# A step of the RWKV-7 recurrence on one core: four state products together, output products and the next first products queued behind them

## The chip, the cores and the metric

The kernel runs on one core of a Trainium2 chip. The metric is the device time of one execution in microseconds (us). Five engines work side by side, each through its own instructions in order, and meet through semaphores: PE (TensorE, matmuls; its weight loads are listed as PEld), DVE (VectorE), ACT (ScalarE), POOL (GpSimd) and SP (SyncE, which issues the transfers). Only PE writes products, into PSUM; DVE and ACT take them from there.

## The reference

Two decoder layers over 1024 tokens of width 1024. Layer 0 mixes time with the RWKV-7 recurrence, 16 heads of 64 by 64 state; layer 1 attends with a forget gate. Each has an MLP of squared ReLU behind it. The recurrence is what the change touches:

```python
def step(S, inp):
    r_t, w_t, k_t, v_t, a_t, b_t = inp
    sa = jnp.einsum('bhvk,bhk->bhv', S, a_t)
    S = S * w_t[:, :, None, :] + sa[..., :, None] * b_t[..., None, :] + v_t[..., :, None] * k_t[..., None, :]
    y = jnp.einsum('bhvk,bhk->bhv', S, r_t)
    return S, y
...
x = x + (1.0 + gt1) * y
h = modulate(rms_norm(x, norm_mlp_g[i]), sh2, sc2)
x = x + (1.0 + gt2) * sq_relu_mlp(h, mlp_up[i], mlp_down[i])
```

## The kernel before, in words

The recurrence is done in chunks of 64 tokens. A unit (`units`) is four heads (two pairs, `q` = 0 and 1; `e` = 0 and 1 are the two heads of a pair) over 256 tokens, so four chunks; there are 16 units, and so 64 steps `c`. What can be had without the state is made ahead by `early` and `late` for the units to come. The rest is serial, and it is `chain`. A step of it has five kinds of product, four small matmuls (64 columns) each, one for each `q` and `e`; letters are used for them from here on:

- **A**: state by the decayed keys, into a tile `pq` (line 888; a helper's line, so rows show it as L875 `pq<-st,ar` or `pq<-sv,ar`). DVE adds `xk` and writes `xs` (line 892).
- **Y**: state by the receptance, into the output bank `py` (line 890; L875 `py<-ar,st`).
- **T**: the solved triangle `tt` by `xs`, into `pq` (line 897; L875 `pq<-xs,tt`). ACT and DVE copy the halves to `uv` (lines 898, 899).
- **B**: the new part of the state, `bkt` by `uv`, into `pq` (line 906). DVE scales it and adds the decayed old state (lines 908 and 910), one instruction for each `q`; POOL makes the decayed copy `sp` for the next step (line 867).
- **O**: the part of the output from within the chunk, `uv` by `sc`, into `py` (line 915).

The trace shows each of these matmuls as two records: x8 in one of its rows are the four matmuls of one kind in a step.

`pq` is one bank with one buffer: each new product into it waits for the reader of the last. In the code of before, the loop over `q` holds two B's and then DVE's update of that `q`, twice over. The steps of the recurrence are short, so other work is put between them: at each `yield` of `chain`, `units` runs a few pieces of the preparation, of the gating of the unit before and of dense work (`beside`: projections, then the MLP of the first 512 tokens). `tc.issue_after` queues these pieces behind the chain's instruction on its engine. The dense work is `mm3` (lines 124, 126, 128): three matmuls of 512 columns for a product, on weights that `load_w` brings and splits in two (lines 115 to 117). A scheduler sets the final order of each engine's instructions from priorities and these edges; the chain has high priority, which lets its ready instructions go first but doesn't hold two of them together.

Of the kernel before, what the change touches and what calls it, by code (L numbers as in the profile page):

```python
# [75 lines left out]
class K:  # L76
# [596 lines left out]
    def phase_wkv(self, es, rest, done):  # L673


        tc, nc, ap = self.tc, self.nc, self.ap
        V, S, G, PE = nc.vector, nc.scalar, nc.gpsimd, nc.tensor
        ident = self.cst("ident")
        H = (slice(0, 64), slice(64, 128))
# [3 lines left out]
        def where(u):  # L683

            j, g, q = u // 8, u % 8 // 2, u % 2
            return j, 2 * g, slice(j * HT + q * 256, j * HT + (q + 1) * 256)
# [5 lines left out]
        def lng(n, shape, bufs=2):  # L692
            return pool["s"].tile(shape, F32, name=n, tag=n, bufs=bufs)
# [4 lines left out]
        def bank(n, bufs=1):  # L698
            return (self.pe if n == "pe" else pool["p"]).tile([128, 512], F32, name=n, tag=n, bufs=bufs)
# [151 lines left out]
        def chain(u, w):  # L851

            j, p, ts = where(u)
            ar, uv, sc, xk, bkt, tt, pc = (w[n] for n in ("ar", "uv", "sc", "xk", "bkt", "tt", "pc"))
            yp = bank("py")
            old = self.sv[:, p:p + 2]
            begin, end = ts.start == 0, ts.stop == T
            of = lambda a: a.rearrange("p (q c) d -> p q c d", q=2)
            pc, xk = pc.rearrange("p (q c) -> p q c", q=2), of(xk)
            us = [of(uv[0:64, :, e]) for e in range(2)]  # L860

            def small(n, bufs=2):
                return lng(n, [128, 2, HD], bufs)

            def scaled(st, c):
                sp = small("sp")
                G.tensor_tensor(out=sp, in0=st, in1=pc[:, :, c:c + 1].broadcast_to([128, 2, HD]), op=ALU.mult)
                return sp

            def state():  # L870
                return bank("pq")[:, 0:128].rearrange("p (q d) -> p q d", q=2)

            def both(ps, lhs, rhs, start, stop):
                for e in range(2):
                    ins = PE.matmul(out=ps[H[e]], lhsT=lhs[H[e]], rhs=rhs[H[e]], start=start, stop=stop)  # L875
                return ins


            st = None if begin else old
            sp = None if begin else scaled(old, 0)  # L880
            for c in range(4):
                first, last = begin and c == 0, end and c == 3
                ys = [yp[:, (q * 4 + c) * HD:(q * 4 + c + 1) * HD] for q in range(2)]
                xs = xk[:, :, c]
                if not first:
                    ps = state()
                    for q in range(2):
                        ins = both(ps[:, q], ar[:, 0, q * 4 + c], st[:, q], True, True)
                    for q in range(2):
                        both(ys[q], st[:, q], ar[:, 1, q * 4 + c], c + q == 0, False)  # L890
                    x = small("xs")
                    ins2 = V.tensor_tensor(out=x, in0=ps, in1=xs, op=ALU.add)
                    xs = x
                    yield ins, ins2
                ps = state()
                for q in range(2):
                    ins = both(ps[:, q], tt[:, q * 4 + c], xs[:, q], True, True)
                S.copy(out=us[0][:, :, c], in_=ps[H[0]])
                yield ins, V.tensor_copy(out=us[1][:, :, c], in_=ps[H[1]])
                ins2 = None  # L900
                if not last:
                    ps = state()
                    st = small("st", 3) if c < 3 else old
                    for q in range(2):
                        for e in range(2):
                            PE.matmul(out=ps[H[e], q], lhsT=bkt[:, q * 4 + c, e], rhs=uv[:, q * 4 + c, e], start=True, stop=True)
                        if first:
                            ins2 = V.tensor_scalar(out=st[:, q], in0=ps[:, q], scalar1=pc[:, q, c:c + 1], scalar2=None, op0=ALU.mult)
                        else:
                            ins2 = V.scalar_tensor_tensor(out=st[:, q], in0=ps[:, q], scalar=pc[:, q, c:c + 1], in1=sp[:, q], op0=ALU.mult, op1=ALU.add)  # L910
                    if c < 3:
                        sp = scaled(st, c + 1)
                for q in range(2):
                    for e in range(2):
                        ins = PE.matmul(out=ys[q][H[e]], lhsT=uv[:, q * 4 + c, e], rhs=sc[:, q * 4 + c, e, 1], start=first and q == 0, stop=c + q == 4)
                yield ins, ins2
            w["y"] = y = lng("y", [128, W], 1)
            S.copy(out=y, in_=yp)
# [42 lines left out]
        def units(beside):  # L961
# [13 lines left out]
            for u in range(2 * KT):  # L975
                def prep():
                    if self.EF and u + 2 < 2 * KT:
                        yield from early(u + 2, ws[u + 2])
                    if u + 1 < 2 * KT:
                        yield from late(u + 1, ws[u + 1])  # L980
                    if not self.EF and u + 2 < 2 * KT:
                        yield from early(u + 2, ws[u + 2])
                pg = prep()
                gens = [[pg, self.PR, 0.0], [last, self.NG8 if u == 8 else self.NG, 0.0], [beside, self.NA if u < self.UA else self.NC if u < self.UC else self.NB, 0.0]]
                ch = chain(u, ws[u])
                while True:
                    with tc.high_priority():
                        ins = next(ch, None)
                    if ins is None:
                        break  # L990
                    with ExitStack() as ea:
                        for i in ins:
                            if i is not None and self.GATE:
                                ea.enter_context(tc.issue_after(i.ins))
                        step(gens)
                self.drain(pg)
                self.drain(last)
                last = gate(u, ws[u])
# [471 lines left out]
```

## Time and profile before

| what | value |
|---|---|
| median of 3 runs | 3394.25 us (3393.43 to 3404.93) |
| the profiled execution's own time | 3394.05 us |
| its span | 3392.1 us, 50350 instructions |
| PE busy | 3214.4 us (95%) |
| PEld, DVE, ACT, POOL busy | 72%, 57%, 42%, 40% |
| the recurrence | its first copy (L898) starts at 333.2 us, its last O (L915) at 1303.3 us |

The span is what the trace covers; the execution's time is 1.95 us more. Busy PE is not PE at its peak, since the ends of matmuls are modelled and overlap: how long a matmul holds PE up is read from the starts of the next ones.

### The profile page before, as it was taken

The page shows a single profiled execution, that of the slowest core. Times are in us where ns is not written, and L with a number is a line of the kernel's source. Part 1 is how long each engine was busy: PE and PEld are TensorE (multiplying, and loading weights), DVE is VectorE, ACT ScalarE, POOL GpSimd, SP SyncE. Part 2 cuts the span into 40 slices and gives each one's busy share as a digit, 9 for nine tenths or more (in the row PEclk, how much of TensorE's full clock was granted, in tenths as well). Part 3 has the DMA queues.
Part 4 walks back from the last instruction along what each step waited for, and adds up shares of the span by engine and source line. Part 5 has one row for each costly group of instructions (what it writes and reads, how often), then busy time and mean ns, then how long its engine had stood idle before and what let it go on. Part 6 is the DMA issues. An engine that isn't in the chain of part 4 may idle for free.

```text
span 3392.1 us, 50350 instructions
## 1 busy us (share of the span) xinstructions
PE 3214.4 (95%) x19108; PEld 2438.4 (72%) x19108; DVE 1943.0 (57%) x3239; ACT 1432.8 (42%) x2284; POOL 1358.7 (40%) x868
## 2 busy tenths in 40 slices
PE   4898999999999999899999999999999999999997
PEld 2456666666777776678887777777778888778886
DVE  7496765766556534167786433555566666454344
ACT  3642236523433223242233556667555544332323
POOL 3364432333333233354444432444423333454444
PEclk7899999899999999899999999999999999999999
DMA  7374344355333223236752233666544443232222
GB/s 276 98 234 151 95 128 135 116 152 150 88 102 102 85 76 125 68 111 224 229 187 88 85 131 119 207 203 182 177 128 136 144 134 100 88 111 95 98 98 83
DMA packets 294065, 452.90 MB, mean 134 GB/s; under 512 B 114720, under 2 KB 170432, under 8 KB 293824
## 3 DMA queue, kind: packets, MB, share of 16 engines
q1 hardware_dynamic: 293824, 449.68, 42.3%
q8 instruction: 152, 2.49, 0.3%
q14 instruction: 89, 0.73, 0.1%
HBM read 371.25 MB, written 78.32 MB: 133 GB/s over the span
## 4 chain that ended last, share of the span: by engine, by line
PE 50%; DVE 4%; ACT 2%; DMA 1%; issue 1%; POOL 1%; SPq 0%; DVEq 0%; ACTq 0%; POOLq 0%
PE pj L124 8%; PE pj L128 7%; PE pj L126 7%; PE pk L128 7%; PE pk L124 7%; PE pk L126 7%; PE pt L1328 2%; PE po L1313 1%; PE po L1314 1%; PE ps L1285 1%; PE ps L1286 1%; DVE t L239 1%; DVE hl L241 1%; DVE x L1016 1%; DVE modacc L185 0%
## 5 line engine op out<-in xcount | busy, mean ns | idle before, releaser
L117 POOL TENSOR_TENSOR wl<-wraw,wh 128x1024 fp32r<-128x1024 f32 x385 | 947.7, 2462 | 1231.7 <-ACT wh L116 1162.6
L116 ACT CAST wh<-wraw 128x1024 fp32r<-128x1024 f32 x385 | 402.6, 1046 | 822.0 <-PE pk L126 359.2
L124 PE MATMUL pj<-hh,wh 128*128 128x512 f32 x1120 | 448.6, 408 | 7.4 <-DVE sq L1090 2.7
L128 PE MATMUL pj<-hh,wl 128*128 128x512 f32 x1120 | 445.1, 403 | 5.5 <-POOL wl L117 5.5
L126 PE MATMUL pj<-hl,wh 128*128 128x512 f32 x1120 | 443.2, 401 | 0.0
L1016 DVE SCALAR_TENSOR_TENSOR x<-pj,G,x 128x512 f32<-128x512 f32 x304 | 225.8, 747 | 164.3 <-PE pj L128 162.2
L128 PE MATMUL pk<-hh,wl 128*128 128x512 f32 x688 | 272.1, 402 | 8.6 <-POOL wl L117 8.6
L124 PE MATMUL pk<-hh,wh 128*128 128x512 f32 x688 | 270.2, 398 | 8.9 <-ACT wh L116 7.8
L126 PE MATMUL pk<-hl,wh 128*128 128x512 f32 x688 | 267.3, 395 | 0.0
L124 PEld LDWEIGHTS pj<-hh,wh 128*128 128x128 f32 x1120 | 210.9, 189 | 61.9 <-issue 4.5
L1016 DVE SCALAR_TENSOR_TENSOR x<-pk,G,x 128x512 f32<-128x512 f32 x240 | 176.2, 746 | 135.7 <-PE pk L128 135.2
L128 PEld LDWEIGHTS pj<-hh,wl 128*128 128x128 f32 x1120 | 210.6, 188 | 58.9 <-POOL wl L117 7.7
L126 PEld LDWEIGHTS pj<-hl,wh 128*128 128x128 f32 x1120 | 211.1, 189 | 48.1 <-issue 2.4
L124 PE MATMUL pj<-mh,wh 128*128 128x512 f32 x564 | 236.9, 421 | 6.0 <-DVE mr L1046 3.0
L126 PE MATMUL pj<-ml,wh 128*128 128x512 f32 x564 | 224.3, 398 | 0.0
L128 PE MATMUL pj<-mh,wl 128*128 128x512 f32 x564 | 219.4, 399 | 2.4 <-POOL wl L117 2.4
L124 PE MATMUL pk<-mh,wh 128*128 128x512 f32 x460 | 182.1, 398 | 8.9 <-DVE mr L1046 5.4
L166 ACT CAST mh<-mr 128x512 fp32r<-128x512 f32 x128 | 79.5, 621 | 250.6 <-PE pj L128 109.1
L126 PE MATMUL pk<-ml,wh 128*128 128x512 f32 x460 | 181.7, 395 | 0.0
L185 DVE SCALAR_TENSOR_TENSOR modacc<-modw,cact,modacc 128x1024 f32<-128x1024 f32 x98 | 155.1, 1583 | 31.0 <-DMA modw<-in_modw_dram 22.5
L128 PE MATMUL pk<-mh,wl 128*128 128x512 f32 x460 | 166.6, 397 | 0.0
L124 PEld LDWEIGHTS pk<-hh,wh 128*128 128x128 f32 x688 | 130.7, 190 | 42.8 <-ACT wh L116 11.6
(334 smaller groups left out, 6493.2 us busy)
## 6 DMA issues: line engine op xcount, KB each, us to landing
wraw<-in_up_dram SPq DMA_DIRECT2D x128, 512.0 KB
wraw<-in_down_dram SPq DMA_DIRECT2D x128, 512.0 KB
modw<-in_modw_dram SPq DMA_DIRECT2D x96, 512.0 KB
wraw<-in_wqg_dram SPq DMA_DIRECT2D x32, 512.0 KB
wraw<-in_wk_dram SPq DMA_DIRECT2D x24, 512.0 KB
wraw<-in_wv_dram SPq DMA_DIRECT2D x24, 512.0 KB
x<-in_xT_dram SPq DMA_DIRECT2D x32, 256.0 KB
wraw<-in_wr_dram SPq DMA_DIRECT2D x16, 512.0 KB
```

The costliest lines, as they stand in the source:

```text
L116: nc.scalar.copy(out=wh, in_=raw)
L117: self.weng.tensor_tensor(out=wl, in0=raw, in1=wh.bitcast(F32), op=ALU.subtract)
L124: mm(out=p, lhsT=wh, rhs=hh[k], start=first, stop=False)
L126: mm(out=p, lhsT=wh, rhs=hl[k], start=False, stop=False)
L128: mm(out=p, lhsT=wl, rhs=hh[k], start=False, stop=last)
L166: self.nc.scalar.copy(out=out_h, in_=src)
L185: nc.vector.scalar_tensor_tensor(out=acc, in0=w, scalar=ck, in1=acc, op0=ALU.mult, op1=ALU.add)
L239: nc.vector.scalar_tensor_tensor(out=t, in0=x[k], scalar=A[:, k:k + 1], in1=rs, op0=ALU.mult, op1=ALU.mult)
L241: nc.vector.scalar_tensor_tensor(out=hl[k], in0=t, scalar=sh[:, k:k + 1], in1=hh[k].bitcast(F32), op0=ALU.add, op1=ALU.subtract)
L1016: self.nc.vector.scalar_tensor_tensor(out=x[j][m], in0=ps, scalar=gain[:, m:m + 1], in1=x[j][m], op0=ALU.mult, op1=ALU.add)
L1285: PE.matmul(out=o[:, 0:r], lhsT=qs[:, q], rhs=kh[:, i * n:i * n + r], start=True, stop=False)
L1328: PE.transpose(out=pt[:, i * 256 + b * 128:i * 256 + (b + 1) * 128], in_=Ps[b][:, (k + i) * 128:(k + i + 1) * 128], identity=ident)
```

## The change

B is made for all four first, and DVE's two updates come behind in a loop of their own. Within a step three edges are added on PE: Y is queued behind A, O behind B, and the next step's A behind O. The pieces at the first `yield` are queued behind A as before. No instruction is added or removed: the matmuls, DVE, ACT and POOL instructions of the chain are the same ones with the same operands.

```diff
             st = None if begin else old
             sp = None if begin else scaled(old, 0)
+            ins = None
+
+            def behind():
+
+                return tc.issue_after(ins.ins) if ins is not None else ExitStack()
+
             for c in range(4):
                 first, last = begin and c == 0, end and c == 3
                 ys = [yp[:, (q * 4 + c) * HD:(q * 4 + c + 1) * HD] for q in range(2)]
                 xs = xk[:, :, c]
                 if not first:
                     ps = state()
-                    for q in range(2):
-                        ins = both(ps[:, q], ar[:, 0, q * 4 + c], st[:, q], True, True)
-                    for q in range(2):
-                        both(ys[q], st[:, q], ar[:, 1, q * 4 + c], c + q == 0, False)
+                    with behind():
+                        for q in range(2):
+                            ins = both(ps[:, q], ar[:, 0, q * 4 + c], st[:, q], True, True)
+                    head = ins
+                    with behind():
+                        for q in range(2):
+                            ins = both(ys[q], st[:, q], ar[:, 1, q * 4 + c], c + q == 0, False)
                     x = small("xs")
                     ins2 = V.tensor_tensor(out=x, in0=ps, in1=xs, op=ALU.add)
                     xs = x
-                    yield ins, ins2
+                    yield head, ins2
...
                     for q in range(2):
                         for e in range(2):
-                            PE.matmul(out=ps[H[e], q], lhsT=bkt[:, q * 4 + c, e], rhs=uv[:, q * 4 + c, e], start=True, stop=True)
+                            ins = PE.matmul(out=ps[H[e], q], lhsT=bkt[:, q * 4 + c, e], rhs=uv[:, q * 4 + c, e], start=True, stop=True)
+                    for q in range(2):
                         if first:
                             ins2 = V.tensor_scalar(out=st[:, q], in0=ps[:, q], scalar1=pc[:, q, c:c + 1], scalar2=None, op0=ALU.mult)
...
-                for q in range(2):
-                    for e in range(2):
+                with behind():
+                    for q, e in ((0, 0), (0, 1), (1, 0), (1, 1)):
                         ins = PE.matmul(out=ys[q][H[e]], lhsT=uv[:, q * 4 + c, e], rhs=sc[:, q * 4 + c, e, 1], start=first and q == 0, stop=c + q == 4)
```

What it does to the order. On PE, before, the second half of B in a step of unit 13 (it is the step that the rows below show from 1105 us on), between two dense matmuls (rows are line, operation, output and operands, columns; x is a count):

```order
L126 MATMUL pj<-ml,wh 128x512
L906 MATMUL pq<-uv,bkt 64x64
L875 MATMUL py<-ar,st 64x64
L906 MATMUL pq<-uv,bkt 64x64
L875 MATMUL py<-ar,st 64x64
L128 MATMUL pj<-mh,wl 128x512
```

Two B's stand in turn with two Y's; the first two B's are in another place, ahead of these by several dense matmuls, with the O's.

On PE, in the changed kernel, the B's of a step in the same part of the program (L915 is now B, L925 is O):

```order
L124 MATMUL pj<-hh,wh 128x512
L915 MATMUL pq<-uv,bkt 64x64 x4
L925 MATMUL py<-sc,uv 64x64 x4
L126 MATMUL pj<-hl,wh 128x512
L128 MATMUL pj<-hh,wl 128x512
```

All four B's stand together, and all four O's right behind.

On PE, before, A in that step:

```order
L124 MATMUL pj<-mh,wh 128x512
L875 MATMUL pq<-st,ar 64x64 x4
L875 MATMUL py<-ar,st 64x64 x2
L126 MATMUL pj<-ml,wh 128x512
L128 MATMUL pj<-mh,wl 128x512
```

Only two Y's are left to go with A. In the changed kernel:

```order
L126 MATMUL pj<-ml,wh 128x512
L875 MATMUL pq<-st,ar 64x64 x4
L875 MATMUL py<-ar,st 64x64 x4
L128 MATMUL pj<-mh,wl 128x512
L124 MATMUL pj<-mh,wh 128x512
```

Four Y's follow four A's.

On DVE, before, the two updates of the state in one of the last units (L910), among residual updates of the MLP (L1016):

```order
L1016 SCALAR_TENSOR_TENSOR x_7389<-pj,G,x_7389 128x512
L910 SCALAR_TENSOR_TENSOR st<-pq,pc,sp 128x64
L1016 SCALAR_TENSOR_TENSOR x_7390<-pj,G,x_7390 128x512
L803 TENSOR_TENSOR sc<-pl,cs 128x4x128 x2
L910 SCALAR_TENSOR_TENSOR st<-pq,pc,sp 128x64
L1016 SCALAR_TENSOR_TENSOR x_7391<-pj,G,x_7391 128x512
```

On DVE, in the changed kernel, in that unit (L920 is the update, L1026 the residual, L901 the sum that A feeds):

```order
L1026 SCALAR_TENSOR_TENSOR x_7386<-pj,G,x_7386 128x512
L920 SCALAR_TENSOR_TENSOR st<-pq,pc,sp 128x64 x2
L1026 SCALAR_TENSOR_TENSOR x_7387<-pj,G,x_7387 128x512
L1026 SCALAR_TENSOR_TENSOR x_7388<-pj,G,x_7388 128x512
L901 TENSOR_TENSOR xs<-pq,sc 128x128
```

The two updates stand side by side, where other work of DVE stood between them.

## Rows read from the trace of the kernel before

**Rows 1.** Windows: stretch, us; busy PE, PEld, DVE, ACT, POOL; clock; DMA.

```profile
330.00:1305.00 975.00, 950.33 (x8630) 665.73 (x8630) 572.39 (x1273) 362.00 (x565) 336.28 (x269) 0.98 0.38 112
330.00:650.00 320.00, 305.87 (x3091) 206.96 (x3090) 214.53 (x489) 145.70 (x226) 118.56 (x106) 0.96 0.42 120
```

**Rows 2.** PE's waits from 330 to 1305: total us, times, longest.

```profile
PE pj L126 <- DVE xl L167: 8.0, 4, 4.5
PE pq L875 <- DVE st L910: 3.9, 2, 2.9
```

**Rows 3.** PE in order of time (start, us): half of B with Y.

```profile
1105.24 0.40 PE L126 MATMUL pj<-ml,wh 128*128 128x512 f32 x1
1105.57 0.33 PE L906 MATMUL pq<-uv,bkt 128*64 128x64 f32 x2
1105.83 0.32 PE L875 MATMUL py<-ar,st 64*64 64x64 f32 x2
1106.08 0.33 PE L906 MATMUL pq<-uv,bkt 128*64 128x64 f32 x2
1106.34 0.33 PE L875 MATMUL py<-ar,st 64*64 64x64 f32 x2
1106.60 0.49 PE L128 MATMUL pj<-mh,wl 128*128 128x512 f32 x1
1106.93 0.40 PE L124 MATMUL pj<-mh,wh 128*128 128x512 f32 x1
...
1107.40 0.40 PE L128 MATMUL pj<-mh,wl 128*128 128x512 f32 x1
```

**Rows 4.** PE in order of time: eight small matmuls in one group.

```profile
1107.72 0.68 PE L715 MATMUL pe<-ar,bk 64*64 64x64 f32 x16
1108.34 0.50 PE L124 MATMUL pj<-mh,wh 128*128 128x512 f32 x1
```

**Rows 5.** PE in order of time: A with two Y's.

```profile
1109.14 0.40 PE L124 MATMUL pj<-mh,wh 128*128 128x512 f32 x1
1109.46 0.45 PE L875 MATMUL pq<-st,ar 64*64 64x64 f32 x8
1109.75 0.28 PE L875 MATMUL py<-ar,st 64*64 64x64 f32 x4
1109.96 0.50 PE L126 MATMUL pj<-ml,wh 128*128 128x512 f32 x1
```

**Rows 6.** PE in order of time: the other half of B with O.

```profile
1119.67 0.40 PE L124 MATMUL pj<-hh,wh 128*128 128x512 f32 x1
1120.00 0.27 PE L915 MATMUL py<-sc,uv 128*64 128x64 f32 x1
...
1120.50 0.50 PE L126 MATMUL pj<-hl,wh 128*128 128x512 f32 x1
```

**Rows 7.** PE in order of time: an O by itself.

```profile
1280.51 0.40 PE L128 MATMUL pj<-mh,wl 128*128 128x512 f32 x1
1280.84 0.33 PE L915 MATMUL py<-sc,uv 128*64 128x64 f32 x2
1281.10 0.49 PE L124 MATMUL pj<-mh,wh 128*128 128x512 f32 x1
```

**Rows 8.** PE's groups from 330 to 1305: busy us, mean ns, idle before.

```profile
L906 PE MATMUL pq<-uv,bkt 128*64 128x64 f32 x480 | 59.5, 247 | 3.7 <-DVE uv L899 1.8 <-DVE st L910 1.1 <-DVE st L908 0.3
L875 PE MATMUL py<-ar,st 64*64 64x64 f32 x384 | 46.1, 233 | 0.0
L915 PE MATMUL py<-sc,uv 128*64 128x64 f32 x512 | 44.8, 232 | 1.4 <-ACT uv L898 1.4
L875 PE MATMUL pq<-xs,tt 64*64 64x64 f32 x480 | 27.6, 231 | 0.1
```

**Rows 9.** DVE in order of time: updates of the state; idle before.

```profile
1104.64 0.75 DVE L1016 SCALAR_TENSOR_TENSOR x<-pj,G,x 128x512 f32<-128x512 f32 x1 [0.30 <-PE pj L128]
1106.45 0.28 DVE L910 SCALAR_TENSOR_TENSOR st<-pq,pc,sp 128x64 f32<-128x64 f32 x1 [1.06 <-PE pq L906]
```

## The prediction

> **What bounds the kernel now.** I first cut the span where the recurrence stands, from 330 to 1305 us. There PE is busy for 950.33 of 975 us; DVE has 572.39, ACT 362.00 and POOL 336.28 [rows 1]. So the stage is PE's. Busy PE is not PE at its peak, however, so the next question was what PE does in these 950 us, and whether the chain makes it wait. PE's waits in the stage, summed by who ended them, say no: the longest is that of the dense split on DVE with 8.0 us, and A's wait for the new state in a unit's later steps is 3.9 us, 2 times [rows 2]. The scheduler finds enough other work to put between the chain's hops. A shorter chain as such is therefore worth little here.
>
> What the chain does cost is PE's own time, and that is seen only in the order of time, from the start of the dense matmul ahead of a small group to the start of the one behind it. Dense matmuls start 0.235 us apart (two of them from 1106.93 to 1107.40), and what a gap has beyond that is the price of the group in it [rows 3]. Half of B in turn with half of Y takes from 1105.24 to 1106.60, 1.36 us, so 1.125 us for four small matmuls [rows 3]. Four A and two Y take from 1109.14 to 1109.96, so 0.585 us for six [rows 5]. The other half of B with four O's takes from 1119.67 to 1120.50, so 0.595 us for six [rows 6]. Eight preparation matmuls of the same size, all of one kind, take from 1107.40 to 1108.34, so 0.705 us for eight [rows 3, 4]. From six to eight that is 0.06 us for each more in a group. The four in turn are nearly five times as dear as four more in a group (0.24 us).
>
> Why they are dear stands in the same rows. B, Y, B, Y start at 1105.57, 1105.83, 1106.08 and 1106.34: each takes 0.26 us by itself [rows 3]. In the group of eight the first to the last take 0.62 us up to the dense start behind them, 0.078 us each [rows 4]. A B has the shape 128*64 and a Y 64*64 (the numbers behind the operands), so in the turn the shape changes at every matmul, and none has a neighbour of its own kind to run beside.
>
> **The change part by part.** Nothing is added or removed; groups are put together. Counting over PE's whole order of before, there are 48 places with B and Y in turn, 7 with two B's and then two Y's, and 31 O's by themselves, the rest of their step being elsewhere. In the order of the changed kernel there are none of the first two, and two lone O's; 54 of the 60 B groups are four B's with four O's, and 53 of the A groups are four A's with four Y's. Six pairs of B's stand alone in either order, so they cancel.
>
> - *The 48 turns.* Their matmuls become two more B's in a group with O and two more Y's in a group with A: 0.24 us in place of 1.125, 0.885 saved each, 42.5 us.
> - *The 7 with two and two.* No row here shows one. It lies between 0.24 (as part of a group) and 1.125 (in turn); with one change of shape, not three, it is nearest to the six-matmul groups, 0.59. I take 0.6, so 0.36 saved each, 2.5 us (bounds 0 and 6.2).
> - *The lone O's.* One costs from 1280.51 to 1281.10, 0.59 less 0.235, so 0.355 us [rows 7]; in a group 0.06. For 29 fewer of them that is 8.6 us.
> - *Given back.* In four steps of the changed order Y doesn't stand right behind A. Two groups of four at 0.465 (0.585 less two times 0.06) for one of eight at 0.705 is 0.225 more, 0.9 us.
>
> 42.5 + 2.5 + 8.6 - 0.9 is 52.7 us.
>
> *A check by another view, which gives the upper bound.* T's four matmuls always stand together: 27.6 us busy for 480 records, so 0.46 us for a step's eight. B has 59.5 for as many, Y 46.1 for 384, O 44.8 for 512 [rows 8]. If each were a group like T, they would have 27.6, 22.1 and 29.4, together 71.3 us less. That counts the ends of groups which now overlap, so it is too much; it is the bound.
>
> *What is put later.* The first of DVE's two updates now comes behind all four B's, 0.12 us later than behind two (two times 0.06); but A needs both, and the second comes much sooner, since before it B's second half stood behind DVE's first update and several dense matmuls. A now stands behind the step's O's, 0.24 us of PE, while DVE runs two updates of 0.28 us [rows 9]: this is hidden, and without that cover it would lengthen the chain by 0.24 us a step, not PE's work. Y behind A delays nobody, since T is not queued behind Y and the output bank is read only at the unit's end. POOL's copy of the state needs both updates, as before. The chain's transfers are none, so no queue of SP is passed.
>
> [...] The turn shows 0.26 us for each matmul against 0.078 in a group of one shape [rows 3, 4]. [...]
>
> **The time.** The profiled execution took 3394.05 us (span 3392.1 and 1.95 around it), 0.2 below the median of the runs. PE is the stage's bound, so I take PE's saving as the stage's: 3394.05 - 52.7 is 3341 us. Behind the stage the same work is left.
>
> **The rivals.**
>
> [...]
>
> *The waits in it go too.* Some small groups stand behind a DVE result; with one hop fewer in each step these waits may fall away as well. The busy view's bound is 71 us: 3323.
>
> *Another engine paces the stage (no change).* From 330 to 650 DVE is busy for 214.53 of 320 us and PE for 305.87 [rows 1], and PE's longest wait, for the split of the dense operands, is on DVE [rows 2]. If DVE's queue sets the pace of that and the middle third, PE only waits where it worked, and the change saves in the last third alone, a quarter of the steps (15 of 60): 13 us, 3381. Against it: DVE is idle for a third of the time even there, and what PE waits for it is 1% of the stage.
>
> *A stalls PE (slower).* A now has a fixed place behind O, and PE runs its matmuls in order, so when the state is late all dense work behind A waits too. The place is the end of B: two updates of 0.28 us, and ahead of them perhaps one residual update of 0.75 us that DVE took up first [rows 9]; with hops that is up to 1.5 us. In the changed order at least nine other matmuls stand between O and A (in most 14 to 20), which is 2.1 us if they are dense, but only some 0.5 us if they are small ones. It decides against the change when PE waits over 0.88 us (52.7 over 60 steps) on average, and at 1.2 us a step it is 3413. Before, this wait cost 3.9 us in all [rows 2]. [...]
>
> That the change doesn't do what it says is excluded by the order.
>
> **How the numbers follow.** The forecast has 0.60; its own range, by the two-and-two's bounds and some 10 us for a whole order that is scheduled anew, is 3330 to 3352. Only drains 0.14, the waits too 0.10, no change 0.11, slower 0.05. The range reaches from the upper bound with a little scatter, 3315, to the partial case with as much, 3370: it leaves out no change, slower and little else. A measurement of this kernel can tell about 0.5%, 17 us, from no change: faster than that are the first three, 0.84; within it 0.11; slower 0.05.
>
> **What would show it.** Right: PE's small groups are eight in a row at about 0.7 us from dense to dense; B's busy time falls from 59.5 to some 30 us, and Y's and O's together by some 35 to 40; the recurrence's last O starts some 50 us sooner or more; PE's waits in the stage stay near 25 us. Wrong: groups of eight that cost over 0.9 us (only drains), longer waits of PE for the split (DVE paces), or waits of A for the state of tens of us (slower). An error of my own would be a stage that shrinks and a later one that grows, by transfers or weights that come in another order.

## The result, and the profile after

The changed kernel takes 3373.77 us (median of 4 runs, 3368.51 to 3374.93) against 3396.16 us of the kernel before (4 runs): a ratio of 0.9925, with a 95% interval of 0.991 to 0.994. It is faster by some 22 to 25 us, where the forecast was 53 us with a range of 3315 to 3370 us. The profiled execution took 3374.93 us, 1.2 us above the median. Two executions, one of 3911.14 us at a granted clock of 0.73 and one of 4428.66 us at 0.648, are left out of the medians below.

The first place to look is the top of the profile's page: span and busy time of the changed kernel.

```profile
span 3373.2 us, 50399 instructions
PE 3166.2 (94%) x19108; PEld 2413.8 (72%) x19108; DVE 1954.5 (58%) x3239; ACT 1432.9 (42%) x2284; POOL 1349.0 (40%) x868
```

PE's busy time fell from 3214.4 to 3166.2 us, by 48.2. The span fell only from 3392.1 to 3373.2, by 18.9. So PE is idle for 207.0 us (3373.2 less 3166.2) where it was idle for 177.7: 29.3 us of what the change freed were not used. Where they lie is read from windows that cut both spans at the same places. The kernel before (columns as in [rows 1]):

```profile
0.00:330.00 330.00, 253.85 (x1093) 157.67 (x1094) 225.97 (x297) 135.99 (x187) 154.38 (x111) 0.84 0.57 189
330.00:980.00 650.00, 628.83 (x6106) 433.45 (x6106) 419.96 (x972) 264.80 (x417) 231.91 (x202) 0.97 0.43 124
980.00:1383.00 403.00, 388.76 (x2773) 282.24 (x2774) 177.76 (x335) 118.99 (x177) 129.92 (x79) 0.98 0.30 94
```

The same windows of the changed kernel:

```profile
0.00:330.00 330.00, 250.00 (x1098) 156.33 (x1099) 230.69 (x299) 135.99 (x187) 153.71 (x112) 0.86 0.57 190
330.00:980.00 650.00, 603.55 (x6173) 420.46 (x6172) 429.89 (x977) 265.88 (x419) 228.18 (x206) 0.96 0.43 124
980.00:1383.00 403.00, 384.65 (x2763) 282.11 (x2764) 172.99 (x331) 122.64 (x180) 133.91 (x78) 0.97 0.31 95
```

And two more of the changed kernel, the last third of the recurrence and the whole of it:

```profile
980.00:1263.00 283.00, 282.64 (x2384) 206.18 (x2384) 140.53 (x287) 89.22 (x136) 93.25 (x59) 1.00 0.30 92
330.00:1263.00 933.00, 886.19 (x8556) 626.64 (x8554) 570.43 (x1264) 355.10 (x555) 321.43 (x265) 0.97 0.39 115
```

From 330 to 980 us, the first two thirds of the recurrence, PE's idle time went from 21.2 (650 less 628.83) to 46.45 us (650 less 603.55), and in these 650 us PE got through 6173 records in place of 6106, 1.1% more. So little is gained there: two thirds of the way, at the 321st of B's 480 records, the changed kernel is 7 us ahead (879.9 for 887.3 us), and at the last O 40 us. Of the 29.3 us, 25.3 are here; 3.9 are ahead of the recurrence, 4.1 in the stretch behind 980, and the rest of the span has 4 less. In the last third of the recurrence, by contrast, PE is idle for 0.36 of 283 us.

The groups themselves did what the prediction said. PE's groups from 330 to 1263, where the recurrence now ends (columns as in [rows 8]):

```profile
L915 PE MATMUL pq<-uv,bkt 128*64 128x64 f32 x480 | 29.4, 236 | 9.5 <-DVE uv L908 5.4 <-DVE bkt L848 3.9
L925 PE MATMUL py<-sc,uv 128*64 128x64 f32 x508 | 28.6, 225 | 0.0
L875 PE MATMUL pq<-xs,tt 64*64 64x64 f32 x480 | 28.5, 232 | 2.1 <-DVE xs L901 2.1
L875 PE MATMUL py<-ar,st 64*64 64x64 f32 x384 | 20.3, 220 | 0.0
```

B takes 29.4 us busy where it took 59.5, and Y and O together 48.9 where they took 90.9 [rows 8]. In order of time a step looks like this (the changed kernel, unit 13):

```profile
1115.12 0.40 PE L128 MATMUL pj<-mh,wl 128*128 128x512 f32 x1
1115.44 0.45 PE L915 MATMUL pq<-uv,bkt 128*64 128x64 f32 x8
1115.72 0.40 PE L925 MATMUL py<-sc,uv 128*64 128x64 f32 x8
1116.06 0.51 PE L124 MATMUL pj<-mh,wh 128*128 128x512 f32 x1
...
1118.72 0.40 PE L126 MATMUL pj<-ml,wh 128*128 128x512 f32 x1
1119.04 0.45 PE L875 MATMUL pq<-st,ar 64*64 64x64 f32 x8
1119.32 0.40 PE L875 MATMUL py<-ar,st 64*64 64x64 f32 x8
1119.65 0.50 PE L128 MATMUL pj<-mh,wl 128*128 128x512 f32 x1
```

Four B's and four O's take 0.94 us from dense start to dense start, four A's and four Y's 0.93; less the 0.235 that a dense matmul takes anyway, 0.705 and 0.695 us. That is the 0.705 of the preparation's group of eight [rows 3, 4], and the step's price by which the forecast was made. Summed over the trace, from the start of each small matmul of the chain to the start of the next matmul, the chain holds PE for 157.0 us before and 108.4 after: 48.6 less, where the forecast has 52.7. The same sum over the other matmuls, with PE's idle time taken out, doesn't change: the 10119 matmuls of 512 columns hold PE for 2571.1 us in both kernels, and the preparation with all that is left for 490.5 and 490.4. So what the groups gave was not lost to slower matmuls elsewhere, though the granted clock over the span is 0.967 for 0.970; part of it came back as idle time.

What is new is how often PE waits. The six largest of PE's waits from 330 to 1263 in the changed kernel (columns as in [rows 2]):

```profile
PE pe L715 <- DVE bk L747: 5.9, 4, 2.0
PE pj L126 <- DVE xl L167: 5.8, 7, 1.7
PE pq L915 <- DVE uv L908: 5.4, 7, 2.1
PE pq L915 <- DVE bkt L848: 3.9, 3, 1.9
PE pj L124 <- DVE mr L1056: 3.3, 1, 3.3
PE pq L875 <- DVE st L920: 2.9, 2, 2.6
```

None of them stands out. The view has 52 waits in all, where the recurrence of the kernel before has 25, and in both they are some 0.9 us long on average; the longest here is 3.3 us. They are spread over the preparation (`bk`, `bkt`), the dense operands (`xl`, `mr`) and the chain (`uv`, `st`), and 36 of the view's 46 us are waits for DVE. In the time in which PE is idle from 330 to 980 us, DVE is busy for 83% (over the whole stretch for 66%); in the kernel before it is the same 83%, of 21.2 us. A's wait for the state in a unit's later steps, the one that an extra edge could have made long, is 2.9 us, less than the 3.9 of [rows 2].

### The profile page after: what moved, and what is told of

Same layout as the page of the kernel before. It is cut to its first block, busy times and chain, and to the rows that moved or that the text cites. A ratio compares the mean times of both kernels' runs of the same rounds, so it can differ in the third digit from the quotient of the medians.

```text
span 3373.2 us, 50399 instructions
## 1 busy us (share of the span) xinstructions
PE 3166.2 (94%) x19108; PEld 2413.8 (72%) x19108; DVE 1954.5 (58%) x3239; ACT 1432.9 (42%) x2284; POOL 1349.0 (40%) x868
## 5 line engine op out<-in xcount | busy, mean ns | idle before, releaser
L1026 DVE SCALAR_TENSOR_TENSOR x<-pj,G,x 128x512 f32<-128x512 f32 x304 | 225.9, 747 | 167.9 <-PE pj L128 166.7
L1026 DVE SCALAR_TENSOR_TENSOR x<-pk,G,x 128x512 f32<-128x512 f32 x240 | 176.7, 747 | 139.1 <-PE pk L128 138.6
```

What stands on the lines that cost most here:

```text
L1026: self.nc.vector.scalar_tensor_tensor(out=x[j][m], in0=ps, scalar=gain[:, m:m + 1], in1=x[j][m], op0=ALU.mult, op1=ALU.add)
```

## The experiments

Times are medians, and kernels are compared by the ratio to the kernel before on the same chip. PE's idle time from 330 to 980 us is quoted beside most: 21.2 before, 46.45 after. It is read from one profiled execution of each kernel. The texts of expectation name theories by number. Theory 1, the *pace* theory: in the first two thirds another engine, DVE with the preparation on it, sets the pace, so that PE's saving turns into waiting there. Theory 2, the *edges* theory: the new edges hold PE's order fixed and so make it wait. Theory 3, the *order* theory: the waits come from the order that the scheduler happened to make, not from DVE's load. Theories 4 and 5 come with the last pair: the edge from A to Y makes PE wait, or the idle time comes with groups that cost less PE time, whatever holds them together.

**Each half of the change alone.** The first kernel only regroups B, the second only has the edges:

```diff
# e1_regroup: the kernel before, and in it
                         for e in range(2):
                             PE.matmul(out=ps[H[e], q], lhsT=bkt[:, q * 4 + c, e], ...)
+                    for q in range(2):
                         if first:
# e2_edges: the changed kernel, and in it
-                    for q in range(2):
                         if first:
```

> Only the first part of the change: four B's together, DVE's updates behind them; none of the three edges. In PE's order the 48 turns of B and Y are gone, 29 O's still stand alone. By my prices PE's small groups then cost some 43 us less than before. Theory 1 (in the first two thirds of the recurrence PE has caught up with DVE's in-order queue, so part of what PE saves becomes waiting): PE's idle time from 330 us to the last O rises by some 20 us as in the changed kernel, and the kernel is 15 to 22 us faster than before. Theory 2 (the edges hold PE's order fixed and so make it wait): idle time stays near the 25 us of before and the kernel is 35 to 43 us faster.

> Only the second part: the three edges; B stays in two halves with DVE's updates between. The order has no turns, but 58 halves of B alone, at 0.23 us more than in a group (13 us), so small groups cost some 38 us less than before. Theory 1: part of it becomes waiting, 12 to 20 us faster than before. Theory 2 (edges make PE wait): PE's idle time as in the changed kernel or more, since A hangs on one more hop, 0 to 15 us faster.

Regrouping alone takes 3379.67 us, ratio 0.9945 (0.9931 to 0.9959); the edges alone 3378.6, 0.9939 (0.9928 to 0.9951). Each gives some 19 to 21 us (the pace theory had 15 to 22 and 12 to 20), and both together 25: they don't add up. Without any edge the kernel doesn't reach the 35 us of the edges theory, so the edges alone are not what eats the saving. By the sum over starts, regrouping saves 33 us (123.7 for 157.0) and the edges 31 (126.0). Window of the kernel that only regroups:

```profile
330.00:980.00 650.00, 612.95 (x6175) 429.05 (x6173) 423.14 (x976) 267.21 (x421) 232.61 (x206) 0.96 0.43 124
```

And of the one that has only the edges:

```profile
330.00:980.00 650.00, 616.27 (x6255) 426.51 (x6254) 429.00 (x982) 267.45 (x421) 235.22 (x207) 0.96 0.43 125
```

PE is idle for 37.1 and 33.7 us: each half raises the idle time by itself, by 16 and 12.5, and both together by 25.

**Less work on DVE.** Twelve of the 15 rounds of the triangular solve (`tm`, `ti` on DVE) are left out in both kernels, so these two don't compute the reference's output:

```diff
-            for s in range(15):
+            for s in range(3):
```

> The changed kernel with 12 of the 15 rounds of the small triangular solve on DVE left out (24 short instructions for each of 16 units; the output is not the reference's). That takes DVE work away in the first two thirds and no PE work. Theory 1: PE's idle time falls from 47 to 20 us or less, time near 3350. Theory 3 (the waits come from the order that the scheduler happened to make, not from DVE's load): idle time stays above 35 us, time 3365 to 3375.

> The same left out in the kernel before. Theory 1: before, PE had less to wait for; idle time falls from 25 to about 12 us, time 3382 to 3388, so that the change is worth 32 us or more between these two. Theory 3: the change is worth the same 22 us between these two as with all rounds.

The changed kernel goes to 3352.68 us (0.9860, 0.9848 to 0.9873), the kernel before to 3404.22 (1.0022, 1.0003 to 1.0041). The first looks like the pace theory, which gave 3350 for it, and misses the order theory's 3365 to 3375; but the idle time, which was to fall to 20 us or less, is still 37.5. Window of the changed kernel with three rounds:

```profile
330.00:980.00 650.00, 612.50 (x6278) 428.14 (x6279) 366.45 (x691) 271.60 (x425) 232.43 (x204) 0.95 0.44 124
```

DVE is 63 us less busy there than in the changed kernel (366.45 for 429.89), and PE's idle time fell by 9; of the 21 us gained another 7 lie ahead of the recurrence, where PE is idle for 73.4 of the first 330 us in place of 80.0. The kernel before, for which 3382 to 3388 us were expected, got nothing at all from the same cut, and its idle time rose to 28.0. Between these two the change is worth 55 us, which is the "32 us or more" of the pace theory and not the 22 of the order theory. So each theory has one part of this pair for it and one against.

**More work on DVE.** An independent instruction of 128x256 on DVE behind every round of pieces in units 0 to 9. The expectation counts 120 of them; the trace has 116, since four units have one round less:

```diff
                         step(gens)
+                        if u < 10:
+                            V.tensor_tensor(out=spare, in0=spare, in1=carry[:, 0:256], op=ALU.mult)
```

> The changed kernel with idle DVE work added: one 128x256 product on a spare tile at each of the 120 turns of units 0 to 9, about 0.35 us each by the nearest row (half of a 128x512 at 0.68), 42 us in all; nothing waits for it. Theory 1 (DVE's queue paces the first two thirds): most of it is paid, 25 to 40 us slower than the changed kernel, near 3400. Theory 3 (waits come from the order made, DVE has room): 0 to 12 us slower.

> The same work added to the kernel before. Theory 1: PE is nearer to being the bound there, so less is paid than in the changed kernel, 8 to 20 us. Theory 3: 0 to 12 us, like the other.

One takes 0.576 us on average in the changed kernel and 0.577 in the kernel before; the 116 have 66.8 and 66.9 us, where the expectation has 42. The changed kernel pays 25 us by the medians (3398.76; 1.0003, 0.9991 to 1.0015), though its profiled execution took 3383.73, only 9 us more than the changed kernel's; the kernel before pays about 39 by the ratio (3436.78; 1.0116, 1.0094 to 1.0137). The first is what the pace theory gave (25 to 40 us, near 3400), the second is not (8 to 20), and the order theory (0 to 12 us for both) missed both. If DVE set the pace in the changed kernel and not in the one before, the second should have paid less. But the two did not get the same load: over the span DVE's busy time rose by 42.9 us in the changed kernel (1997.4 for 1954.5) and by 73.8 in the kernel before (2016.8 for 1943.0), so that each paid a little over half of what was added. The pair doesn't decide against the pace theory.

**More dense work beside the chain in the first units.** `NA` and `NC` are the rates at which `units` hands out dense pieces in units 0 to 6 and 7 to 9:

```diff
-    NA = 2.2
+    NA = 2.6
-    NC = 3
+    NC = 3.6
```

> The changed kernel with more dense work put beside the first ten units: 2.6 pieces a turn in place of 2.2 for units 0 to 6, 3.6 in place of 3 for units 7 to 9; the later units have less of it. Theory 1: PE has idle time in the first two thirds, and dense work of the last third, where PE has none, moves into it: 12 to 22 us faster than the changed kernel, near 3355. Theory 3: the time stays within 8 us of the changed kernel's.

> The same rates in the kernel before, where PE has some 20 us idle in the first two thirds in place of 46. Theory 1: 3 to 9 us faster than before. Theory 3: within 8 us of before, to either side.

The changed kernel falls to 3335.73 us (0.9826, 0.9798 to 0.9853), the kernel before stays at 3401.7 (0.9999, 0.9984 to 1.0014; its profiled execution took 3386.43). No theory had so much for the changed kernel: 12 to 22 us by the first, under 8 by the third; and the 3 to 9 us that the first had for the kernel before didn't come. With these constants the change is worth 0.0173, 59 us. But the gain isn't where the idle time of the recurrence is: from 330 to 980 PE is still idle for 44.8 us. It is behind the recurrence. The changed kernel there, from the end of the recurrence, and inside it:

```profile
1263.00:1383.00 120.00, 102.02 (x382) 75.93 (x382) 32.46 (x44) 33.43 (x44) 40.66 (x19) 0.91 0.31 102
...
1323.00:1343.00 20.00, 14.69 (x49) 10.71 (x48) 1.50 (x2) 3.20 (x4) 6.47 (x4) 0.84 0.17 53
```

What PE waits for in these 120 us (the changed kernel's waits):

```profile
PE pk L128 <- POOL wl L117: 7.0, 5, 1.7
PE pk L124 <- ACT wh L116: 4.8, 5, 1.0
```

The weights of the dense work, which ACT and POOL split as PE needs them. With the higher rates the stretch is full:

```profile
1263.00:1383.00 120.00, 119.29 (x513) 94.19 (x512) 40.93 (x58) 41.95 (x55) 55.98 (x26) 1.00 0.39 129
```

131 more records in the same 120 us, at the full granted clock in place of 0.91. At 0.235 us for a dense matmul they are 31 us, about the gain of 34 us by the ratio. So this gain is another one than the one that was lost. The kernel before fills that stretch too with these rates, but they move the last O of its recurrence from 1303.3 to 1325.7 us; in the changed kernel, whose groups are shorter, it moves only from 1263.2 to 1267.5.

Two kernels asked whether more can be had in the same way: rates of 3.0 and 3.6, and the rates of 2.6 and 3.6 with some of DVE's splits moved to POOL.

> As the changed kernel with more dense work early, but 3.0 pieces a turn in units 0 to 6. The gain with 2.6 came from the stretch behind the recurrence, where PE had waited for weights. If that stretch is all there was, 3.0 brings nothing more: 3335 to 3350. If PE's idle time in the first third is also filled by it, 3320 to 3332.

> The changed kernel with 2.6 pieces a turn, and the low halves of the dense operands of the second 512 tokens made by POOL in place of DVE (32 products, about 0.88 us each off DVE, 1.35 on POOL). Theory 1: DVE has 28 us less in the first third, PE waits less, 5 to 15 us faster than with 2.6 pieces alone (3340). Theory 3: within 6 us of that; if POOL's weight splits hold the operands up, slower.

```diff
# e12_dense_pool
-            self.split(a, b, x)
+            self.split(a, b, x, nc.gpsimd if half else V)
```

They take 3341.94 us (0.9835, 0.9819 to 0.9851) and 3345.37 us (0.9854, 0.9839 to 0.9869), and from 330 to 980 PE is idle for 39.8 and 40.6. Neither more dense work nor fewer splits on DVE takes more than 4 to 7 us off the idle time there, and neither makes the kernel faster than the rates of 2.6 and 3.6 do. That was expected of the first if the stretch behind the recurrence is all that there is (3335 to 3350); of the second the pace theory had 5 to 15 us more of gain.

**The rate of the preparation.** `PR` is the rate at which the preparation's pieces are handed out, 2.2 in both kernels; 2.6 lets it run further ahead, 1.9 less far:

> The kernel before with the preparation put in faster, 2.6 pieces a turn in place of 2.2; no work added. It makes the scheduler find another order for the same work. Theory 3 (the constants of before fit the order of before; any other order pays more for the preparation's small groups and waits): 5 to 25 us slower than before. Theory 1 (DVE's load sets the pace, whatever the order): within 8 us of before.

> The same constant in the changed kernel. Theory 3: somewhere within 15 us of the changed kernel, to either side, and 35 to 60 us faster than the other of this pair. Theory 1: the pair differs by 22 us as before.

> The kernel before with the preparation put in slower, 1.9 pieces a turn. Theory 3: 5 to 25 us slower than before. Theory 1: within 8 us.

> The same constant in the changed kernel. Theory 3: 35 to 60 us faster than the other of this pair. Theory 1: 22 us faster.

The kernel before takes 3407.39 us at 2.6 (1.0032, 1.0018 to 1.0045) and 3411.41 at 1.9 (1.0040, 1.0028 to 1.0053); the changed kernel 3376.85 (0.9933, 0.9918 to 0.9948) and 3373.94 (0.9926, 0.9909 to 0.9942). Either way the kernel before loses 11 to 14 us, as the order theory had it (5 to 25), and the changed one hardly 3. So 2.2 fits the order of the kernel before, and the changed kernel doesn't mind; at 1.9 the change would have been worth 39 us. The pairs differ by 34 and 39 us, just under and at the lower end of the 35 to 60 that the order theory had; the pace theory had the 22 us of the change as it is. The idle time explains the loss in part only. The kernel before at 1.9:

```profile
330.00:980.00 650.00, 619.66 (x6014) 427.51 (x6012) 412.54 (x930) 263.06 (x414) 225.68 (x199) 0.96 0.42 122
```

It has 30.3 us, 9 more than with its own constant; the changed kernel at 1.9 has 47.5, as ever.

**Is PE's idle time slack?** A is issued five times over, into the same place with the same result, in units 0 to 9 (first kernel) or 10 to 15 (second):

```diff
-                        for q in range(2):
+                        for q in [0, 1] * (5 if u < 10 else 1):
                             ins = both(ps[:, q], ar[:, 0, q * 4 + c], st[:, q], True, True)
```

> The changed kernel with A's four matmuls issued five times over in units 0 to 9 (the same products into the same place): 16 more small matmuls in 36 steps, 0.06 us each in a group, so 34 us more work for PE in the first two thirds of the recurrence, and none for another engine. Theory 1 (there PE has caught up with what DVE and ACT feed it, and part of its time is waiting): half or less is paid, 5 to 18 us slower than the changed kernel, and PE's idle time before 980 us falls from 46 by 12 or more. Theory 3 (PE is the bound there too, the missing gain is the cost of another order): all is paid, 30 us or more slower.

> The same in units 10 to 15 alone: 24 steps, 23 us more for PE in the last third, where PE has no idle time. Both theories: paid in full, 19 to 27 us slower than the changed kernel.

The first adds 576 matmuls (1152 records more), which at 0.06 us each are 35 us. It takes 3404.72 us (1.0019, 1.0006 to 1.0032), 31 or 32 us over the changed kernel: nearly all of it is paid. The second adds 384, 23 us, and takes 3389.36 (0.9981, 0.997 to 0.9992), 16 to 19 us more, at or under the lower end of the 19 to 27 expected. The pace theory had at least half of the early ones hidden, and that did not come. Window of the first:

```profile
330.00:980.00 650.00, 605.40 (x7062) 433.70 (x7060) 398.14 (x924) 260.26 (x407) 221.41 (x198) 0.94 0.42 119
```

And its A's there, in PE's groups:

```profile
L875 PE MATMUL pq<-st,ar 64*64 64x64 f32 x1232 | 44.8, 223 | 3.9 <-DVE st L920 2.0 <-DVE tm L772 1.4 <-DVE ti L773 0.5
```

44.6 us are idle, as in the changed kernel, and none of them took up the added work. So the idle time took nothing of work in this place. The place is the chain itself, however. The added A's also delay DVE's sum `xs` and everything that hangs on it, by some 0.96 us a step (an estimate, 16 times 0.06), and a pace set by the chain's hops would have made the kernel pay as much. Added PE work on which nothing waits was not tried.

**Which edge.** Regrouped B's with the edge from B to O alone, Y and the next A being free:

```diff
# e13_o_edge: the changed kernel, and in it
-                    with behind():
-                        for q in range(2):
-                            ins = both(ps[:, q], ar[:, 0, q * 4 + c], st[:, q], True, True)
+                    for q in range(2):
+                        ins = both(ps[:, q], ar[:, 0, q * 4 + c], st[:, q], True, True)
                     head = ins
-                    with behind():
+                    with ExitStack():
# e14_o_dense: the same with NA = 2.6 and NC = 3.6
```

> The changed kernel with one edge alone, O behind B; Y is free again, and its matmuls, of A's shape, stand ahead of A, behind it or by themselves. (The edge of A behind O changes no row of any engine's order, so it isn't tried by itself.) Small groups cost about what they cost in the changed kernel, within 5 us. Theory 4 (holding all four Y's behind A moves work to where PE would have had to cover a wait, so the edge is what makes PE idle): PE's idle time before 980 us falls from 46 to 38 or less, 5 to 12 us faster than the changed kernel. Theory 5 (idle time comes with small groups that cost less PE time, whatever holds them together): idle 42 to 48, within 5 us of the changed kernel.

> The same with 2.6 and 3.6 pieces of dense work a turn, as the candidate for the best kernel. Theory 4: 3328 to 3335. Theory 5: 3335 to 3345, like the one with all edges.

The first takes 3376.86 us (0.9949, 0.9933 to 0.9966); its profiled execution took 3386.43 us, above that. From 330 to 980 PE is idle for 49.2 us, where theory 4 had 38 or less and theory 5 42 to 48, so the waits don't come from the edge from A to Y. The edge from O to the next A moves no row: with it or without it PE's order is the same. What is left when both are taken off is the regrouped B with O behind it, and that has the full idle time. Its window:

```profile
330.00:980.00 650.00, 600.76 (x6098) 415.48 (x6097) 430.80 (x969) 263.39 (x417) 227.45 (x204) 0.96 0.43 123
```

The second has the lowest ratio of this study: 3333.51 us (3330.88 to 3337.13), ratio 0.9816 (0.9803 to 0.9829). That is inside theory 4's 3328 to 3335, but the idle time, by which theory 4 explained it, is 42.4 us. Its stretch behind the recurrence is filled like that of the kernel with the rates alone, and its interval meets that one's, so that it is better than the 3335.73 us of that kernel isn't settled:

```profile
1263.00:1383.00 120.00, 119.34 (x508) 94.45 (x507) 41.24 (x58) 41.17 (x55) 56.12 (x27) 1.00 0.38 128
```

**The pairs side by side.** What the change is worth, as the ratio before less the ratio after, in each setting (1% is 34 us), and PE's idle time from 330 to 980 us. By the intervals of the two ratios the worth is known to some 5 to 11 us either way:

| setting in both kernels | before | after | the change is worth | idle before | idle after |
|---|---|---|---|---|---|
| as they are | 1 | 0.9925 | 25 us (22 by the medians) | 21.2 | 46.45 |
| preparation 2.6 | 1.0032 | 0.9933 | 34 us | 28.7 | 44.4 |
| preparation 1.9 | 1.0040 | 0.9926 | 39 us | 30.3 | 47.5 |
| dense 2.6 and 3.6 | 0.9999 | 0.9826 | 59 us | 34.0 | 44.8 |
| 3 rounds of the solve | 1.0022 | 0.9860 | 55 us | 28.0 | 37.5 |
| 116 more on DVE | 1.0116 | 1.0003 | 38 us | 45.2 | 57.2 |

With the constants as they are it is worth least, though 34 and 38 us are hardly apart from 25 by these intervals. The forecast's 53 us lie inside the spread. The idle time rises with the change in every setting, but by 9.5 to 17 us in the other five and by 25 in the setting as it is: the kernel before, as it was, had less idle time than with any other setting.

## Why the prediction was wrong

- *The prices held.* The forecast for a turn was "0.24 us in place of 1.125": groups of eight cost 0.705 and 0.695 us, and the chain's hold on PE fell by 48.6 us of the 52.7 worked out. PE's busy time over the whole span fell by 48.2, B's to 29.4 ("some 30"), Y's and O's together by 42.0 ("some 35 to 40"). No run shows the price behind *only drains*, the case with the chance of 0.14 from which the range has its upper end of 3370 us. What the runs showed in its place is that four B's, with their 128 rows, and four O's cost the 0.705 us of the preparation's group of eight, so the row of that group was the right guide.
- *The step that failed:* "PE is the stage's bound, so I take PE's saving as the stage's." PE's saving was there and the stage's wasn't. PE's waits in the recurrence, which were to "stay near 25 us", rose from 24.7 to 46.8 us (933 less 886.19), all of it in the first two thirds; the last O came 40 us sooner (1263.2 for 1303.3), not 50. Behind it PE was idle for 18.0 us up to 1383, most of it waiting for weights, where it had been idle for 10.7 from 1303; ahead of the recurrence there were 3.9 us more, and in the rest of the span 4 less. 48.2 us less busy and 29.3 more idle make the 18.9 us of the span.
- *Another engine paces the stage* had the picture nearly right (7 of the 40 us by which the last O comes sooner are gained in the first two thirds, and most of PE's new waits are on DVE), and its time of 3381 is nearer than the forecast. Its cause is neither shown nor excluded. Against it: added PE work in those units is paid nearly in full, and taking 63 us off DVE takes only 9 off PE's idle time. For it: the same cut makes the changed kernel 21 us faster and the kernel before none. The pair with more work on DVE doesn't decide.
- *A stalls PE* is excluded: A's wait for L920's state is 2.9 us in all. *The waits go too* is the opposite of what came.
- *The width was wrong as well.* "Some 10 us for a whole order that is scheduled anew" is too little. The same change is worth 25 to 59 us when a rate or some filler work is set otherwise. Any of three other settings of the rates leaves the changed kernel within 3 us of where it is or makes it faster, while it makes the kernel before 0 to 14 us slower: the profile before was that of an order for which the rates fit, and its 21 us of idle time are not a property of the stage (28 to 45 with any other setting). I read them as one. How near a forecast comes in this kernel is therefore partly luck: with the dense rates changed, the same 53 us would have looked right, and part of that gain comes from filling a stretch that the forecast did not speak of.
- *What stays open* is why. The new waits are there in every kernel that has B regrouped with O behind it, whatever the rates and the engines' load (37 to 57 us, for 21 to 45 of the kernels before), and with either half of the change alone there are some of them (37.1 and 33.7). They are many, of about 1 us, mostly on results of DVE. They are not a lack of dense work, and not one edge's. Two readings are left. One is that the scheduler, once the groups are larger, places the other work so that it comes later; no run shows it, and a kernel with the order of the changed one's other work held fixed wasn't tried. The other is that DVE's work comes later: from 330 to 980 us DVE is busy for 9.9 us more with five instructions more (429.89 for 419.96), and two groups of the same instructions take longer there. The kernel before, and then the changed one:

```profile
L773 DVE TENSOR_TENSOR ti<-ti,tm 64x15 f32<-64x15 f32 (+4 forms) x180 | 43.2, 240 | 4.3
L167 DVE TENSOR_TENSOR xl<-t,xh 128x512 fp32r<-128x512 f32 x24 | 19.7, 825 | 0.3 <-ACT xh L166 0.2
```

```profile
L773 DVE TENSOR_TENSOR ti<-ti,tm 64x15 f32<-64x15 f32 (+4 forms) x180 | 49.4, 274 | 4.6
L167 DVE TENSOR_TENSOR xl<-t,xh 128x512 fp32r<-128x512 f32 x24 | 24.9, 1036 | 0.0
```

Why they take longer, and whether PE's waits come from it, no run shows.

## What to carry to other kernels

What a group of small matmuls costs is read from dense start to dense start, and such prices can be carried to the changed kernel: 48.6 of 52.7 us came. That PE's saved time becomes the kernel's does not follow from PE being 95% busy when a scheduler places the work and rates of filler are fitted to the old order; take the saving as what PE no longer does, and say how much of it could come back as idle time spread over many short waits. Before such a change is judged, run both kernels with a rate or two changed: here the change alone gave 0.75%, and together with two constants set anew 1.7 to 1.8%, which the constants alone did not give the kernel before.

## What the runs showed of the hardware

- Eight small matmuls of the shape 128*64, four B's and four O's, cost PE 0.705 us as a group, as much as eight of 64*64 (0.705 in [rows 3, 4], 0.695 for four A's and four Y's).
- PE's busy time showed this cost in its total (48.2 us, as the starts have it), but not in its share, 95% and 94%: a turn of single small matmuls is counted as busy (the four in turn in [rows 3] hold PE for 1.125 us, with no idle time among them).
- Where dense work waits for weights that are split as it goes, PE is busy for 14.69 of 20 us and the granted clock there is 0.84 (the changed kernel, 1323 to 1343 us); with the stretch filled (e7_dense_after) the 120 us show 1.00 in place of 0.91, and hold 513 records in place of 382. The rates that fill it gained 34 us, more than the whole change.
- 116 independent instructions on DVE, which is busy for 65 to 66% of the time from 330 to 980 us, took 0.576 and 0.577 us each on average; they raised DVE's busy time by 42.9 us in one kernel and by 73.8 in the other, and cost these 25 and 39 us, in a stage in which PE, without them, is busy for 93 to 97% of the time.
